# A two-layer decoder trunk on one core: the causal products of the first layer on 64-token pieces and four 64x64 tiles

## The chip, the cores and the metric

The program runs on one core of a Trainium2 chip. The core has a matrix engine (TensorE, "PE" in the profile; its weight loads are listed as "PEld"), a vector engine (VectorE, "DVE"), an activation engine (ScalarE, "ACT"), a general engine (GpSimd, "POOL"), and queues that start DMA transfers from HBM (mostly that of SyncE, "SP"). Each engine works through its own list of instructions in order, and semaphores tie the lists together. The metric is the device time of one execution in microseconds (us), the median of several runs.

## The reference, cut to what matters

256 tokens of width 2048 go through two layers, in float32. The first is a Mamba-2 mixer: a projection gives z, xs, B, C and dt; xs, B and C pass a short convolution and a SiLU. The 64 heads (64 wide) lie in 8 groups of 8 heads; the heads of a group share B and C (128 states). With da the decay per token and head, the output of a head is

```
cb    = C · B^T                                    (256 x 256, one per group)
decay = exp(sum of da over (s, q])   for s <= q    (one per head)
y[q]  = sum over s <= q of cb[q,s] * decay[q,s] * (dt[s] * xs[s])
```

The reference does this in chunks of 128 tokens with a carried state; the kernel forms the causal 256 x 256 products directly. Then follow a skip term, the gate silu(z), a group norm and the output projection. The second layer is sliding-window attention (window 128, 32 query heads over 4 key heads, a sink term), gated and projected out. Both layers end in a layer norm over the residual.

## The kernel before, in words

All weights are streamed once. A unit is 1 MB of a weight matrix: two DMAs (`load_half`, L169), a rounded copy by ACT (`wh`, L178) and the remainder by DVE (`wl`, L181). Every large product is three products of rounded and remainder parts: `mac` (L265) for the projections into z, xs, B, C, q and the gate, and `out_unit` (L339) for the output projections. Units are prepared ahead of their use, in the order of the list `srcs`.

The first layer is a sequence of blocks of 128 columns (`SEQ`): per group the blocks B, C, four of xs, four of z. A plan (`at(t, fn, ...)`, `beside`, `between`) puts the small work of a group behind certain blocks. For group g that is:

- `load_decay` (L534): DMAs that spread the summed decays of four heads over all 128 partitions (tile `rb`). They are issued by POOL for groups 0 to 2 (but one) and by SP after that.
- `sum_decay` (L566) and `exp_decay` (L573), on ACT: the exponent of the decay for each pair of tokens, into tile `e`. Rows (partitions) are the source tokens s of a chunk of 128 and columns are the target tokens q: 256 columns for the first chunk and 128 for the second, 384 per head, 1536 for the four heads of a half group.
- `cb` (L607 and L608): two matmuls, B of a chunk against C, 128x128 stationary, 256 and 128 columns; DVE masks the result into `cbm` (L609).
- `by_cb` (L614), on DVE: `e` times `cbm`, for four heads at once.
- `turn_first` (group 0, L625 and L629) or `turn_xs`, `carry_xs`, `scale_xs` (L641, L651, L657): xs with tokens on partitions, times dt, into tile `xd`.
- `ymm` (L670): for every pair of heads and chunk, `xd` (128 tokens x 64) stationary against `e`. The two heads of a pair go to the two halves of the output partitions, so that two matmuls run on two 128x64 column tiles of PE. DVE takes the result out with a scale (L675) and adds the skip term (L681).
- `gate` (L686 to L701), on POOL, ACT and DVE, then the norm of the group and, a group later, its output projection.

`turn_dt` (L487 to L497) prepares the decays with tokens on partitions (`rtk`, `dtx`). float32 operands that are not in the rounded format take two passes of PE: each such matmul stands in the profile as two instructions.

In the second layer `attend(j, h)` forms the scores (L1209, L1216), DVE and ACT the softmax; `weigh` (L1248 to L1251) and `turn_far` (L1258) divide by the sum and transpose; `rest` calls both. For the pairs (j, h) in `BEHIND_HALF`, `rest` is put off to the next output block. `gate_block` ends each of its blocks with a product on DVE (L1185). At the very end columns 512 to 2047 of rows 0 to 127 are normalised by `norm_aside` on ACT and POOL (L1426 to L1428), and rows 128 to 255 by DVE, ACT and PE (`last`, L1412 to L1447).

PSUM is split into four tiles `mm` and four tiles `ax`, which are handed out in turn.

Of the kernel before, what the change touches and what calls it, by code (L numbers as in the profile page):

```python
# [8 lines left out]
F32 = mybir.dt.float32  # L9
# [61 lines left out]
NSM = 7  # L71
B_ORDER = [("q", 0), ("g", 0), ("q", 1), ("g", 1), ("q", 2), ("o", 0), ("g", 2), ("q", 3),
# [6 lines left out]
BEHIND_HALF = [(1, 1)]  # L79
# [18 lines left out]
def trunk(ctx: ExitStack, tc: tile.TileContext, A: dict, out: bass.AP, dbg=None):  # L98
# [30 lines left out]
    mask_ssd = cc[:, 256:640]  # L129

    tri = cc[:, 256:384]
# [60 lines left out]
    def load_first():  # L192
# [3 lines left out]
        for tag, n in FIRST:  # L196
            if tag == "xr":
                buf = xr_t
            elif tag == "wr":
                buf = wp.tile([P, 1024], F32, tag="wr", name=nm("first"), bufs=NR)  # L200
            else:
                w, bufs = {"rb": (1024, 2), "e": (1536, 2), "yz": (1024, 1)}[tag]
                buf = ap.tile([P, w], F32, tag=tag, name=nm("first"), bufs=bufs)
            raws += [buf[:, i * FW : i * FW + FW] for i in range(n)]
# [209 lines left out]
    dtx = ap.tile([P, 2, NHD], F32, tag="dtx", name="dtx")  # L414
    rtk = ap.tile([P, 2, 2 * NHD], F32, tag="rtk", name="rtk")
# [68 lines left out]
    def turn_dt(sums, dt, q):  # L484
        pt = ax_tile()
        for i, v in enumerate((sums[:, 0, :], sums[:, 1, :], dt)):
            nc.tensor.transpose(pt[:, i * P : (i + 1) * P], v, ident)  # L487
        nc.scalar.copy(
            rtk[:].rearrange("p c (k h) -> p k c h", k=2),
            pt[:, :256].rearrange("p (k c h) -> p k c h", k=2, c=2),  # L490
        )
        elo = q[:]
        nc.scalar.activation(
            elo[:, :128].rearrange("p (c h) -> p c h", c=2), rtk[:, :, 64:128], AF.Exp, scale=-1.0
        )
        nc.vector.tensor_tensor(
            dtx[:], pt[:, 256:384].rearrange("p (c h) -> p c h", c=2),  # L497
            elo[:, :128].rearrange("p (c h) -> p c h", c=2), ALU.mult,
# [30 lines left out]
    def load_decay(g, hf):  # L529
        rb = ap.tile([P, 4, S], F32, tag="rb", name=nm("rb"), bufs=2)  # L530
# [3 lines left out]
        m = (nc.sync if sp else nc.gpsimd).dma_start(  # L534
            rb[:],
            rscr[h0 : h0 + 4, :]
            .rearrange("h q -> (h q)").partition_broadcast(P)
            .rearrange("p (h q) -> p h q", h=4),
        )
        if sp and g < 2:  # L540
            tc.keep_in_program_order(m)
        rbs[g, hf] = rb
# [13 lines left out]
    def sum_decay(g, hf, first=0, last=4):  # L556

        rb = rbs[g, hf]
        h0 = g * 8 + hf * 4
        if first == 0:  # L560
            es[g, hf] = ap.tile([P, 4, 384], F32, tag="e", name=nm("e"), bufs=2)
        e = es[g, hf]
        for h in range(first, last):
            for c, cols in ((0, slice(0, 256)), (1, slice(256, 384))):

                m = nc.scalar.activation(  # L566
                    e[:, h, cols], rb[:, h, c * P :], AF.Relu, scale=-1.0, bias=rtk[:, c, h0 + h : h0 + h + 1]
# [3 lines left out]
    def exp_decay(g, hf):  # L571
        e = es[g, hf]
        m = nc.scalar.activation(e[:], e[:], AF.Exp, scale=-1.0)  # L573
# [29 lines left out]
    def cb(g):  # L603
        st = gs[g]
        cbm = ap.tile([P, 384], F32, tag="cbm", name=nm("cbm"), bufs=1)
        ps = ax_tile()
        nc.tensor.matmul(ps[:, :256], st.bt[:, :128], st.ct[:], start=True, stop=True)  # L607
        nc.tensor.matmul(ps[:, 256:384], st.bt[:, 128:], st.ct[:, 128:], start=True, stop=True)  # L608
        nc.vector.tensor_tensor(cbm[:], ps[:, :384], mask_ssd, ALU.mult)  # L609
        st.cbm = cbm  # L610

    def by_cb(g, hf):
        e = es[g, hf]
        nc.vector.tensor_tensor(e[:], e[:], gs[g].cbm[:].unsqueeze(1).to_broadcast([P, 4, 384]), ALU.mult)  # L614

    def turn_first(g):

        st = gs[g]
        st.xd = ap.tile([P, 2, 4, P], F32, tag="xd", name=nm("xd"), bufs=1)
        for k in range(2):  # L620
# [5 lines left out]
            for i in (2 * k, 2 * k + 1):  # L626
                o = (i % 2) * S
                hh = g * 8 + 2 * i
                m = nc.vector.tensor_tensor(  # L629
                    st.xd[:, :, i, :].rearrange("p c (h d) -> p c h d", h=2),  # L630
                    ps[:, o : o + S].rearrange("p (c h d) -> p c h d", c=2, h=2),
                    dtx[:, :, hh : hh + 2].unsqueeze(3).to_broadcast([P, 2, 2, 64]), ALU.mult,
                )
                pinned(m, True)

    def turn_xs(g):
# [6 lines left out]
        st.xd = ap.tile([P, 2, 4, P], F32, tag="xd", name=nm("xd"), bufs=1)  # L643

    def carry_xs(g, js):

        st = gs[g]
        z = st.zx[:].rearrange("p i (c j) b -> p j c i b", c=2)
        for j in js:
            for i in range(4):  # L650
                m = nc.scalar.copy(st.xd[32 * j : 32 * j + 32, :, :, 32 * i : 32 * i + 32], z[32 * i : 32 * i + 32, j])  # L651
                pinned(m, g > 1 and j > 1)

    def scale_xs(g):
        v = gs[g].xd[:].rearrange("p c i (h d) -> p c (i h) d", h=2)
        d = dtx[:, :, g * 8 : g * 8 + 8].unsqueeze(3).to_broadcast([P, 2, 8, 64])
        pinned(nc.vector.tensor_tensor(v, v, d, ALU.mult), g == 0)  # L657

    def ymm(g):
        st = gs[g]  # L660
        st.yz = ap.tile([P, 4, S], F32, tag="yz", name=nm("yz"), bufs=1)
        for k in range(2):
            ps = ax_tile()
            for i in (2 * k, 2 * k + 1):
                o = (i % 2) * S
                for c in range(2):
                    cols = slice(o + c * P, o + S)
                    for r in range(2):
                        e = es[g, i // 2][:, 2 * (i % 2) + r, :]
                        nc.tensor.matmul(  # L670
                            ps[64 * r : 64 * r + 64, cols], st.xd[:, c, i, 64 * r : 64 * r + 64], e[:, 256:] if c else e[:, :256],
                            start=c == 0, stop=c == 1,
# [902 lines left out]
```

## Time and profile before

| | |
|---|---|
| median of 3 runs | 975.67 us (975.39 to 976.33) |
| the profiled execution | 976.57 us, its span 973.9 us |
| mean granted TensorE clock | 0.997 |
| busy PE / DVE / ACT / POOL | 965.6 / 786.3 / 671.2 / 121.4 us |
| `ymm` on PE (L670) | 256 instructions |
| `cb` on PE (L607, L608) | 32 instructions |

The profile follows one execution. Its chain of waits runs from the last instruction back to whatever released each step, so a time that stands in the chain for a PE group is time that the group adds to the end. The list of waits tells for each engine what it stood still for. A busy time of a group is the sum of what its instructions took and overlaps with others on a pipelined engine; the time in the chain does not.

### The profile page before, as it was taken

How to read it: one execution, taken by the hardware profiler on the slowest of the kernel's cores; microseconds unless marked ns; L12 is line 12 of the kernel's file. 1: busy time of each engine (PE TensorE's matmuls, PEld its weight loads, DVE VectorE, ACT ScalarE, POOL GpSimd, SP SyncE). 2: the span in 40 equal slices, each digit the busy share in tenths (PEclk: the TensorE clock that was granted, in tenths of full speed). 3: DMA queues.
4: the chain of work that ended last, by engine and by line, in shares of the span. 5: the costliest groups of instructions: out<-in, count | busy, mean ns of one | idle time of the engine just before them, and what ended most of it. 6: DMA issues, size and time to landing. Idle time of an engine off the chain costs nothing.

```text
span 973.9 us, 18857 instructions
## 1 busy us (share of the span) xinstructions
PE 965.6 (99%) x7332; PEld 894.5 (92%) x7332; DVE 786.3 (81%) x1216; ACT 671.2 (69%) x1282; POOL 121.4 (12%) x203
## 2 busy tenths in 40 slices
PE   9999999999999999999999999999999999999997
PEld 8999989998999999999899899888999988898976
DVE  7888898886977877787797687889977769778777
ACT  7585883884795685587377579567777776784772
POOL 0000303102110310310300121411000000000003
PEclk9999999999999999999999999999999999999999
DMA  9688566575667666576576654568655545466642
GB/s 357 246 299 323 159 216 227 199 245 189 224 191 226 200 208 205 174 233 203 155 254 201 212 186 158 175 194 266 200 174 155 176 152 174 152 193 196 215 132 86
DMA packets 61273, 197.90 MB, mean 203 GB/s; under 512 B 6800, under 2 KB 11328, under 8 KB 60928
## 3 DMA queue, kind: packets, MB, share of 16 engines
q1 hardware_dynamic: 58528, 188.53, 58.9%
q0 software_dynamic: 2048, 7.65, 2.4%
q8 instruction: 57, 0.93, 0.4%
q10 hardware_dynamic: 608, 0.52, 0.2%
q14 instruction: 32, 0.26, 0.1%
HBM read 194.45 MB, written 2.23 MB: 202 GB/s over the span
## 4 chain that ended last, share of the span: by engine, by line
PE 93%; DVE 4%; ACT 2%; issue 1%; DVEq 0%; ACTq 0%
PE mm L265 60%; PE mm L339 25%; PE ax L670 2%; PE mm L1052 2%; DVE wl L181 1%; ACT p L1244 1%; PE ax L607 0%; ACT wh L178 0%; PE mm L406 0%; ACT ptw L1277 0%; ACT pt L1277 0%; PE ax L983 0%; DVE t L1412 0%; PE ax L1209 0%; PE ax L388 0%
## 5 line engine op out<-in xcount | busy, mean ns | idle before, releaser
L181 DVE TENSOR_TENSOR wl<-wr,wh 128x1024 fp32r<-128x1024 f32 (+2 forms) x354 | 391.8, 1127 | 88.2 <-ACT wh L178 86.6
L178 ACT ACTIVATE wh<-wr 128x1024 fp32r<-128x1024 f32 (+2 forms) x354 | 332.8, 974 | 94.9 <-PE mm L265 51.7
L265 PE MATMUL mm<-xH,wh 128*128 128x256 f32 x1280 | 355.4, 278 | 0.0
L265 PE MATMUL mm<-xL,wh 128*128 128x256 f32 x1280 | 354.4, 277 | 0.0
L265 PE MATMUL mm<-xH,wl 128*128 128x256 f32 x1280 | 354.4, 277 | 0.0
L265 PEld LDWEIGHTS mm<-xH,wh 128*128 128x128 f32 x1280 | 240.7, 188 | 1.8 <-issue 0.5
L265 PEld LDWEIGHTS mm<-xL,wh 128*128 128x128 f32 x1280 | 240.6, 188 | 1.0
L265 PEld LDWEIGHTS mm<-xH,wl 128*128 128x128 f32 x1280 | 240.4, 188 | 0.0
L265 PE MATMUL mm<-x1H,wh 128*128 128x256 f32 x512 | 143.1, 280 | 2.1 <-DVE sg L1185 2.1
L265 PE MATMUL mm<-x1L,wh 128*128 128x256 f32 x512 | 142.6, 278 | 0.0
L265 PE MATMUL mm<-x1H,wl 128*128 128x256 f32 x512 | 142.4, 278 | 0.0
L339 PE MATMUL mm<-wh,yH 128*128 128x512 f32 x256 | 100.7, 394 | 0.0
L265 PEld LDWEIGHTS mm<-x1H,wh 128*128 128x128 f32 x512 | 96.9, 189 | 3.6 <-DVE sg L1185 2.4
L339 PE MATMUL mm<-wl,yH 128*128 128x512 f32 x256 | 99.8, 390 | 0.0
L339 PE MATMUL mm<-wh,yL 128*128 128x512 f32 x256 | 99.8, 390 | 0.0
L265 PEld LDWEIGHTS mm<-x1H,wl 128*128 128x128 f32 x512 | 97.0, 190 | 0.0
L265 PEld LDWEIGHTS mm<-x1L,wh 128*128 128x128 f32 x512 | 96.9, 189 | 0.1
L510 DVE SCALAR_TENSOR_TENSOR cv<-mm,pc,cv 128x255 f32<-128x255 f32 x144 | 68.4, 476 | 4.6 <-ACT cv L508 2.5
L686 POOL TENSOR_TENSOR yz<-yz,z 128x256 f32<-128x256 f32 x32 | 26.7, 842 | 259.9 <-DVE yz L681 259.9
L339 PEld LDWEIGHTS mm<-wl,yH 128*128 128x128 f32 x256 | 48.1, 188 | 10.2
L339 PEld LDWEIGHTS mm<-wh,yH 128*128 128x128 f32 x256 | 48.1, 188 | 9.3 <-issue 0.3
L339 PEld LDWEIGHTS mm<-wh,yL 128*128 128x128 f32 x256 | 48.1, 188 | 9.0
(246 smaller groups left out, 1264.4 us busy)
## 6 DMA issues: line engine op xcount, KB each, us to landing
wr<-in_wa SPq DMA_DIRECT2D x154, 512.0 KB, 5.2
wr<-in_wo SPq DMA_DIRECT2D x64, 512.0 KB, 4.5
wr<-in_wq SPq DMA_DIRECT2D x32, 512.0 KB, 4.4
wr<-in_wg SPq DMA_DIRECT2D x31, 512.0 KB, 5.2
wr<-in_wb SPq DMA_DIRECT2D x16, 512.0 KB, 3.8
wr<-in_wb SPq DMA_DIRECT2D x32, 256.0 KB, 4.3
rb<-rscr SPq DMA_DIRECT2D x11, 512.0 KB, 5.3
wr<-in_wkv SPq DMA_DIRECT2D x8, 512.0 KB, 6.0
```

The costliest lines, as they stand in the source:

```text
L178: m = nc.scalar.activation(h[:, sl], v, AF.Copy)
L181: m = nc.vector.tensor_tensor(l[:, sl], v, h[:, sl].bitcast(F32), ALU.subtract)
L265: m = nc.tensor.matmul(ps, a, b, start=first and i == 0, stop=last and i == 2)
L339: pinned(nc.tensor.matmul(ps, a[:, k, hs], (u.h, u.l)[l][:, ks], start=n == 0 and add is None, stop=n == 11), pin)
L510: nc.vector.scalar_tensor_tensor(a[:, sft:], ps[:, : S - sft], w(3 - sft), a[:, sft:], ALU.mult, ALU.add)
L670: nc.tensor.matmul(ps[64 * r : 64 * r + 64, cols], st.xd[:, c, i, 64 * r : 64 * r + 64], e[:, 256:] if c else e[:, :256], start=c == 0, st ...
L686: nc.gpsimd.tensor_tensor(v, v, st.z[i][:], ALU.mult)
L1052: m = nc.tensor.matmul(ps[:], (x1H, x1L, x1H)[i][:, kk, hs], (u.h, u.h, u.l)[i][:, ks], start=(kk, i) == (0, 0), stop=ui == 3 and (k, i) = ...
L1244: nc.scalar.activation(byhead[:, r], byhead[:, r], AF.Exp, bias=ng[:, r : r + 1], accum_out=rs[:, r : r + 1])
```

## The change

The pieces of tokens become 64 long in the first layer. Even pieces (0 and 2) of one member of a head pair and odd pieces lie on opposite partition halves, and for the other member the other way round: tile `e` holds, on each half of the partitions, the 256, 192, 128 and 64 columns of four pieces for two heads (1280 columns instead of 1536).

- `ymm`: 32 matmuls per group instead of 16, each with 64 rows and 64 output rows, so that four 64x64 tiles of PE are in use; the results lie in two PSUM tiles by row half, and both are taken out after all matmuls. The gates go in the order 0, 2, 1, 3.
- `cb`: four matmuls with 64 stationary columns; the products land on the partition half of their piece. DVE masks them in two steps of 64 partitions, and POOL copies each half to the other partition half.
- `load_decay`: two DMAs onto 64 partitions each instead of one onto 128, half the bytes; the tile holds a whole group.
- `turn_dt`: four copies of 64 partitions instead of one of 128, and a small second set of scales (`dtq`) for group 0. `turn_first`: eight products of 64 partitions instead of four of 128. `carry_xs` and `scale_xs`: the same number and size of instructions to other places.
- Second layer: `rest` of attend(3, 0) is put off behind the first gate product of block 3, which is held ahead of it on DVE. At the end, the multiplication of columns 1536 to 2047 of rows 0 to 127 goes from POOL to DVE, behind the statistics of (1, 1), and the addition on POOL after it.

```diff
+PART = [slice(a, a + 256 - 64 * c) for c, a in enumerate((0, 320, 512, 256))]
-BEHIND_HALF = [(1, 1)]
+BEHIND_HALF = [(1, 1), (3, 0)]
...
-        nc.scalar.copy(
-            rtk[:].rearrange("p c (k h) -> p k c h", k=2),
-            pt[:, :256].rearrange("p (k c h) -> p k c h", k=2, c=2),
-        )
...
+        for r, i in ((0, 0), (1, 1), (0, 1), (1, 0)):
+            to = rtk[64 * r : 64 * r + 64, i].rearrange("p k c n -> p (k c n)").rearrange("p (m b) -> p m b", b=2)
+            of = pt[64 * i : 64 * i + 64, :384].rearrange("p (m r b) -> p r m b", r=2, b=2)[:, r]
+            if r == i:
+                nc.vector.tensor_copy(to, of)
+            else:
+                nc.scalar.copy(to, of)
...
     def load_decay(g, hf):
-        rb = ap.tile([P, 4, S], F32, tag="rb", name=nm("rb"), bufs=2)
+        if hf == 0:
+            rbs[g] = ap.tile([P, 2, 2, S], F32, tag="rb", name=nm("rb"), bufs=2)
...
+        for r in range(2):
+            m = (nc.sync if sp else nc.gpsimd).dma_start(
+                rbs[g][64 * r : 64 * r + 64, hf],
+                rscr[h0 + 2 * r : h0 + 2 * r + 2, :]
...
+        for b in range(first // 2, last // 2):
+            n = 4 * g + 2 * hf + b
+            for c in range(4):
                 m = nc.scalar.activation(
-                    e[:, h, cols], rb[:, h, c * P :], AF.Relu, scale=-1.0, bias=rtk[:, c, h0 + h : h0 + h + 1]
+                    e[:, b, PART[c]], rbs[g][:, hf, b, 64 * c :], AF.Relu, scale=-1.0,
+                    bias=rtk[:, c % 2, 0, c // 2, n : n + 1],
...
-        nc.tensor.matmul(ps[:, :256], st.bt[:, :128], st.ct[:], start=True, stop=True)
-        nc.tensor.matmul(ps[:, 256:384], st.bt[:, 128:], st.ct[:, 128:], start=True, stop=True)
-        nc.vector.tensor_tensor(cbm[:], ps[:, :384], mask_ssd, ALU.mult)
+        for c, half, to in ((0, 0, 0), (1, 64, 0), (2, 64, 192), (3, 0, 256)):
+            nc.tensor.matmul(
+                ps[half : half + 64, to : to + 256 - 64 * c], st.bt[:, 64 * c : 64 * c + 64], st.ct[:, 64 * c :],
+                start=True, stop=True,
+            )
+        for r in range(2):
+            rows, at = slice(64 * r, 64 * r + 64), slice(320 * r, 320 * r + 320)
+            nc.vector.tensor_tensor(cbm[rows, at], ps[rows, :320], mask_ssd[rows], ALU.mult)
+        for r in range(2):
+            rows, at = slice(64 * r, 64 * r + 64), slice(320 * r, 320 * r + 320)
+            nc.gpsimd.tensor_copy(cbm[64 - 64 * r : 128 - 64 * r, at], cbm[rows, at])
...
-                m = nc.vector.tensor_tensor(
-                    st.xd[:, :, i, :].rearrange("p c (h d) -> p c h d", h=2),
...
+                for q in range(2):
+                    rows = slice(64 * q, 64 * q + 64)
+                    m = nc.vector.tensor_tensor(
+                        to[:, q], ps[rows, o : o + S].rearrange("p (c h d) -> p c h d", c=2, h=2),
...
+        pss = [ax_tile(), ax_tile()]
         for k in range(2):
-            ps = ax_tile()
...
+            for c in range(4):
+                for r in range(2):
+                    rows = slice(64 * r, 64 * r + 64)
+                    for b in range(2):
                         nc.tensor.matmul(
-                            ps[64 * r : 64 * r + 64, cols], st.xd[:, c, i, 64 * r : 64 * r + 64], e[:, 256:] if c else e[:, :256],
-                            start=c == 0, stop=c == 1,
+                            pss[r][64 * b : 64 * b + 64, k * S + 64 * c : k * S + S], st.xd[rows, k, b, c],
+                            es[g, k][rows, b, PART[c]], start=c == 0, stop=c == 3,
...
-        for i in range(4):
+        for i in (0, 2, 1, 3):
             at(y, gate, g, i)
...
-            nc.vector.scalar_tensor_tensor(
+            m = nc.vector.scalar_tensor_tensor(
                 t[:, p_, :], t[:, p_, :], 1.0, ps[:, :S], ALU.add, ALU.mult
             )
+            pinned(m, bool(behind_gate))
+            while behind_gate:
+                behind_gate.pop()()
...
-            halves.append(rest)
+            (behind_gate if j == 3 else halves).append(rest)
...
-        ordered(nc.scalar.activation(v, v, AF.Identity, scale=sc[h][1][:], bias=nmr[:]))
-        ordered(nc.gpsimd.tensor_tensor(v, v, gb2[0][:, cols(nb)], ALU.mult))
+        if nmr is not None:
+            ordered(nc.scalar.activation(v, v, AF.Identity, scale=sc[h][1][:], bias=nmr[:]))
+            if nb == 3:
+                return
+        ordered((nc.vector if nb == 3 else nc.gpsimd).tensor_tensor(v, v, gb2[0][:, cols(nb)], ALU.mult))
...
+        elif (h, nb) == (1, 1):
+            norm_aside(0, 3, None)
```

More of the change, by code (lines that the diff above doesn't have):

```diff
@@ L411, in first_products @@
         return pss
-    dtx = ap.tile([P, 2, NHD], F32, tag="dtx", name="dtx")
-    rtk = ap.tile([P, 2, 2 * NHD], F32, tag="rtk", name="rtk")
+    dtx = ap.tile([P, NHD // 2, 4], F32, tag="dtx", name="dtx")
+    dtq = ap.tile([P, 2, 2, 8], F32, tag="dtq", name="dtq")
+    rtk = ap.tile([P, 2, 3, 2, NHD // 2], F32, tag="rtk", name="rtk")
     rscr = dram.tile([P, S], F32, tag="rscr", name="rscr")
@@ L556, in sum_decay @@
     def sum_decay(g, hf, first=0, last=4):
-        rb = rbs[g, hf]
-        h0 = g * 8 + hf * 4
         if first == 0:
-            es[g, hf] = ap.tile([P, 4, 384], F32, tag="e", name=nm("e"), bufs=2)
+            e = ap.tile([P, 1408], F32, tag="e", name=nm("e"), bufs=2)
+            es[g, hf] = e[:, :1280].rearrange("p (h q) -> p h q", h=2)
         e = es[g, hf]
-        for h in range(first, last):
-            for c, cols in ((0, slice(0, 256)), (1, slice(256, 384))):
+        for b in range(first // 2, last // 2):
+            n = 4 * g + 2 * hf + b
+            for c in range(4):
                 m = nc.scalar.activation(
-                    e[:, h, cols], rb[:, h, c * P :], AF.Relu, scale=-1.0, bias=rtk[:, c, h0 + h : h0 + h + 1]
+                    e[:, b, PART[c]], rbs[g][:, hf, b, 64 * c :], AF.Relu, scale=-1.0,
+                    bias=rtk[:, c % 2, 0, c // 2, n : n + 1],
                 )
@@ L1146, in trunk @@
     halves = []
+    behind_gate = []
     def rotate(q):
```

81 lines of the change are left out of this document (37 added, 44 removed).

## The prediction

> **What bounds the kernel now.** I read the page first, then the list of what PE waited for.
>
> ```profile
> span 973.9 us, 18857 instructions
> ...
> PE 965.6 (99%) x7332; PEld 894.5 (92%) x7332; DVE 786.3 (81%) x1216; ACT 671.2 (69%) x1282; POOL 121.4 (12%) x203
> ...
> PE 93%; DVE 4%; ACT 2%; issue 1%; DVEq 0%; ACTq 0%
> ```
>
> ```profile
> PE mm L265 <- DVE sg L1185: 2.1, 1, 2.1
> ```
>
> PE is the bound nearly everywhere: it makes up 93% of the chain, and its one wait inside the span is 2.1 us, on the gate product L1185 in the second layer. In the first layer PE waits for nothing, so there only PE's own time counts, unless the change makes a wait. The rows that price it come from the chain of waits in order of time (start, duration, what), where a duration is what a group adds to the end.
>
> ```profile
> 42.85 16.35 PE mm L265 x144
> 59.20 0.43 PE ax L607 x2
> 59.85 16.35 PE mm L265 x144
> ...
> 87.97 2.75 PE ax L670 x32
> 90.72 16.54 PE mm L265 x144
> 107.27 0.34 PE ax L724 x4
> 107.61 0.54 PE ax L607 x2
> ...
> 124.74 5.46 PE mm L265 x48
> ...
> 231.97 2.75 PE ax L670 x32
> 234.72 0.63 PE ax L607 x2
> 235.57 5.47 PE mm L339 x24
> ...
> 732.52 1.46 PE ax L1216 x32
> ...
> 918.35 16.34 PE mm L339 x72
> ```
>
> **Prices of a pass.** L607 is one 256-column matmul of group 0 in two passes: 0.43/2 = 0.216 us a pass. The two 128-column passes of L608 fill the gap behind it: 59.85 - 59.20 - 0.43 = 0.22, 0.110 each. The line through both (0.83 ns a column) gives 0.163 us for 192 columns and 0.057 for 64.
>
> Two column tiles run abreast: 16 passes of 256 and 16 of 128 in pairs make 8 x 0.216 + 8 x 0.110 = 2.61 us, and L670 shows 2.75. Four 64x64 tiles run abreast too: L1216 of the second layer has 32 passes of 192 columns on four tiles; 32/4 x 0.163 = 1.30, and the row has 1.46. What is over, 0.14 and 0.16, is the entry into the tiled state. The way back to the full array costs about 0.20: the 144 matmuls behind L670 take 16.54 against 16.35, and L607 right behind L670 takes 0.63 against 0.43.
>
> **The change, part by part.**
>
> *ymm.* 64 passes per group on four tiles are 16 rounds, four each of 256, 192, 128 and 64 columns: 4 x (0.216 + 0.163 + 0.110 + 0.057) = 2.18, and 0.16 for the entry, 2.34 us instead of 2.75. Eight groups: -3.28 us. Only the 64-column round has no row. Its lower end is the 0.057 of the line; its upper end is that of a 128-column pass, 0.110, near what one-column matmuls behind a 128-wide weight load take (L724, 0.34/4 = 0.085). I take 0.057, since the weight load is half as wide here; the upper end would add 8 x 4 x 0.053 = 1.70.
>
> *cb.* The old pair costs 0.43 + 0.22 = 0.65 in groups 0 and 2, 0.54 + 0.22 = 0.76 in group 1, and 0.63 + 0.22 = 0.85 in groups 3 to 7, where it stands behind ymm and holds the way back. The new one runs on two column tiles, another state than the 64x64 tiles before it, so an entry (0.14) stands before it and the way back (0.20) behind it. In between, pieces 0 and 1 (256 and 192 columns) run side by side, then 2 and 3 (128 and 64); with the passes issued in order the second pass of piece 1 starts with that of piece 0, at 0.216, ends at 0.379, and piece 2 adds 0.220: 0.60. Sum 0.94. Groups 3 to 7: 5 x 0.09; 0 and 2: 2 x 0.29; 1: 0.18; together +1.21 us. Ends: 0.54 if the halves run freely (2 x 0.216 + 2 x 0.057 = 0.546 on one), 0.77 if the two passes of one matmul come before those of the next; no entry at all between the two tiled states at best. That makes +0.03 to +2.57.
>
> *The work beside it.* ACT's and DVE's passes over `e` shrink from 1536 to 1280 columns and the bytes of `rb` halve; no PE wait hangs on them, so this brings nothing. What is added is 8 small products instead of 4 in `turn_first` and two copies more on DVE in `turn_dt`. The first set stands here:
>
> ```profile
> 80.49 1.41 DVE L629 TENSOR_TENSOR xd<-ax,dtx 128x256 f32<-128x256 f32 x4
> ```
>
> Four more at 0.35 make 1.4 us on DVE; the tile is ready at 81.9 and would be at 83.3, and ymm starts at 87.97: hidden. Uncovered, it would be 1.4. The four copies of `turn_dt`, at the same 0.35 on two engines, fall in a stretch where PE runs 144 matmuls from 42.85 without a gap. The second DMA of each `load_decay` queues behind its first on SP or POOL with half the bytes, and its tile no longer waits for the ACT of the half group before. The outgoing ymm results reach DVE only when all rounds are done, up to half of 2.34 later in PE's terms, and POOL's gates start after the two `cbm` copies: the only reader is the output projection a group later (in group 7, which has no copies, three output units later). All taken at nothing.
>
> The tight place is group 1, where `by_cb` stands right behind `cb` on DVE and now waits for POOL's copies:
>
> ```profile
> 119.17 0.55 DVE L609 TENSOR_TENSOR cbm<-ax,cc 128x384 f32<-128x384 f32 x1
> 119.64 0.74 DVE L348 SCALAR_TENSOR_TENSOR xr<-mm,r,xr 128x512 f32<-128x512 f32 x1
> 120.30 1.75 DVE L614 TENSOR_TENSOR e<-e,cbm 128x1536 f32<-128x1536 f32 x1
> 121.97 0.75 DVE L348 SCALAR_TENSOR_TENSOR xr<-mm,r,xr 128x512 f32<-128x512 f32 x1
> 122.63 2.35 DVE L181 TENSOR_TENSOR wl<-wr,wh 128x1024 fp32r<-128x1024 f32 x2
> ```
>
> ```profile
> 117.64 0.55 POOL L534 DMA_DIRECT2D rb<-rscr  x1 [6.50 <-ACT e L566]
> L850 POOL CAST xH<-xH 128x256 fp32r<-128x256 f32 x1 | 1.1, 1105 | 0.0
> ```
>
> Behind `by_cb` stand two halves of weights (L181); the first is done at 123.8 and used by the matmuls from 124.74, a spare of 0.9. A POOL copy costs at most the 1.1 us of L850, the dearest near row: masking (0.45 for its first half) and two copies end 2.65 us after 119.17, 1.52 later than `by_cb` started; it is itself 0.29 shorter (256 of 1536 columns). The weights come up to 1.23 late, PE waits 0.0 to 0.4. I take 0: ACT and DVE have less to do just before.
>
> *The two waits in the second layer.* The wait of 2.1 us is in block 2, and the reordered one in block 3. What L1185 of block 3 does there:
>
> ```profile
> 905.40 0.42 DVE L1185 SCALAR_TENSOR_TENSOR sg<-sg,mm 128x256 f32<-128x256 f32 x1
> ```
>
> It frees one of four `mm` tiles in turn; three more gate blocks pass, and the tile is wanted at 918.35, 12.5 us later. An earlier L1185 helps nobody. What goes behind it, `rest` of attend(3, 0), feeds only products that come after three more output units. Price 0 both ways.
>
> At the end, the chain runs through DVE, and there is a delay:
>
> ```profile
> 956.93 0.75 DVE L1412 SCALAR_TENSOR_TENSOR t<-xr,mv,gb 128x512 f32<-128x512 f32 x1
> 962.00 0.69 DVE L350 TENSOR_TENSOR xr<-xr,mm 128x512 f32<-128x512 f32 x1 [0.90 <-PE mm L339]
> 965.91 1.31 DVE L1412 SCALAR_TENSOR_TENSOR t<-xr,mv,gb 128x512 f32<-128x512 f32 x1
> ```
>
> ```profile
> 965.41 1.27 POOL L1428 TENSOR_TENSOR xr<-xr,gb 128x512 f32<-128x512 f32 x1
> ```
>
> The same instruction takes 0.75 alone and 1.31 while POOL's last addition runs until 966.68. With one multiplication less, POOL is done some 1.3 us earlier, before 965.91; the multiplication fits DVE's idle 0.90 before 962.00 (0.69, as L350); it waits for the third of ACT's three scalings, and L350 of the next columns queues behind it. SP's stores keep their order, and the one concerned leaves earlier. That is -0.56; the lower end is 0, if DVE and POOL get in each other's way there.
>
> **Sum.** -3.28 + 1.21 - 0.56 = -2.63 us on the profiled 976.57 (span 973.9 and 2.67 around it), 973.9. The median of the runs shown is 0.9 below the profiled execution; from it, 975.67 - 2.63 = 973.0. All good ends give -3.28 + 0.03 - 0.56 = -3.81 (971.9), all bad ones -3.28 + 1.70 + 2.57 + 0.4 = +1.4 (977.1).
>
> **Rivals.** (a) The passes in cb do not pair: 8 x 0.17 more, 974.4. Every case of two tiles in the trace has equal columns; none shows 256 beside 192.
>
> [...]
>
> (c) Slower: `by_cb` of group 1 waits not only for the copies but for what stands before them in POOL's queue. The issue of L534 above waited 6.50 us for ACT. If such a wait precedes the copies, the weights come 6.5 - 0.9 - 0.29 = 5.3 us late, and after a stop PE is slow as well:
>
> ```profile
> 835.00:838.50 3.50, 3.50 (x19) 3.50 (x19) 2.00 (x2) 3.41 (x9) 0.00 (x0) 0.52 0.74 247
> ```
>
> In this window behind the 2.1 us wait the granted clock was 0.52, with 19 matmuls where 31 fit at 16.35/144 each: 1.4 us lost. Together 973.0 + 5.3 + 1.4 = 979.7. It decides from a wait of 3.2 us on (4.6 with the clock: 2.63 to undo and 1.95 beyond). Against it: `rb` has a tile for each group now, so the issue has nothing to wait for.
>
> (d) The wait of block 2 goes after all, with its slow clock: 2.1 + 1.4 less, 969.5. Nothing in the change touches attend(2, 0).
>
> **How the numbers follow.** The sum has a chance of 0.66 (its own range 972.0 to 974.0, of it 0.60 past the bound), (a) 0.11, (b) 0.06, (c) 0.11, (d) 0.04, and 0.02 for a smaller loss elsewhere. 0.2% is 1.95 us, about what a measurement here can tell from no change. Faster is 0.60 + 0.04; the same (973.7 to 977.6) is 0.06 from the sum with (a) and (b); slower is (c) and the rest. The range 971.3 to 975.4 leaves out (c) and (d) and holds (a) and (b).
>
> **What would show it.** L670's successor at 2.3 us per group in the chain, x64; the cb lines at about 0.74 behind it and the next group 0.2 longer; no PE wait near 120 to 130; the 2.1 us wait unchanged; the first L1412 at the end at 0.75. Wrong would be: rounds of the 64x64 tiles longer than the line, or a new PE wait.

## The result, and the profile after

The changed kernel is slower: 980.4 us median of 7 runs (978.22 to 981.65), against 976.06 of the kernel before on the same chip. The ratio is 1.004, with a 95% interval of 1.0031 to 1.005. The forecast was 973.0. The profiled execution took 981.65 us, the longest of the 7; its span is 6.0 us longer than that of before (973.9), where the medians differ by 4.3.

The page of after, its first line, the busy times, and the engines' shares of the chain that ended last:

```profile
span 979.9 us, 19511 instructions
...
PE 968.3 (99%) x7620; PEld 898.6 (92%) x7620; DVE 791.5 (81%) x1232; ACT 664.9 (68%) x1284; POOL 124.7 (13%) x223
...
PE 82%; DVE 5%; issue 4%; DMA 4%; ACT 3%; POOL 1%; ACTq 0%; SPq 0%; DVEq 0%; POOLq 0%
```

PE was 93% of the chain before and is 82% now; DMA, which had no share, has 4%. The list of what PE waited for shows where (total, times, longest):

```profile
PE ax L741 <- POOL sq L709: 2.5, 1, 2.5
PE mm L265 <- DVE sg L1203: 2.0, 1, 2.0
PE mm L265 <- DVE wl L181: 1.1, 1, 1.1
```

The wait on the gate product (L1203, L1185 before) is the old one. Two are new: the norm of group 0 (L741, L724 before) waits for POOL's gate products, and a block near 52 us waits for its weights. The chain of waits of after, followed back from 130 us in order of time (start, duration, what), tells how they hang together:

```profile
44.77 6.48 DMA wr<-in_wa
...
52.23 0.41 ACT ct L519
...
55.20 7.29 DMA wr<-in_wa
...
70.33 0.39 DVE cbm L619
...
111.29 0.74 POOL sq L709
112.03 0.04 issue
112.08 1.02 PE ax L741 x4
113.09 1.26 PE ax L613 x6
114.35 7.61 PE mm L339 x24
```

Before, PE itself was this chain from 42 us on. Now two weight loads (`wr`) of 6.5 and 7.3 us stand in it, DVE's `cbm` of group 0 comes at 70.33, and POOL's last square ends at 112.03, when PE has been standing for 2.5 us. Behind the stop, the product of B and C (L613) takes 1.26 us and the 24 matmuls of L339 take 7.61; in group 3 and after they take 0.69 and 5.67. The granted clock behind the stop is in the windows of after (stretch, its length; then busy time and number of instructions on PE, PE's weight loads, DVE, ACT and POOL; granted clock, DMA share, GB/s):

```profile
45.00:50.00 5.00, 5.00 (x47) 5.00 (x46) 3.17 (x6) 1.78 (x2) 4.00 (x7) 1.00 0.94 238
50.00:55.00 5.00, 4.11 (x37) 3.91 (x35) 2.27 (x4) 3.20 (x6) 0.00 (x0) 1.00 1.04 319
...
112.00:116.00 4.00, 3.92 (x16) 3.41 (x17) 3.52 (x5) 0.35 (x2) 0.02 (x1) 0.50 0.61 186
```

The same windows of before:

```profile
45.00:50.00 5.00, 5.00 (x47) 5.00 (x46) 5.00 (x10) 4.28 (x8) 0.00 (x0) 1.00 0.96 385
50.00:55.00 5.00, 5.00 (x47) 5.00 (x46) 3.63 (x5) 4.31 (x9) 0.00 (x0) 1.00 1.07 321
```

The DMA engines are as busy in both, 0.94 and 0.96 of their time at 45 to 50 us, but they moved 238 GB/s instead of 385 there; at 50 to 55 us the rates are equal. ACT worked 1.78 us instead of 4.28 in the first stretch, DVE 2.27 instead of 3.63 in the second. The waits of after between 40 and 62 us name it:

```profile
ACT wh L178 <- DMA wr<-in_wa: 5.7, 4, 4.5
DVE ct L520 <- ACT ct L519: 4.5, 1, 4.5
```

ACT stood 4.5 us for one weight buffer; the longest such wait of before in this stretch is 1.7. The activation of `ct` is queued behind that weight half on ACT, and DVE's next work behind `ct`.

The parts that were priced came out like this, in the chain of after between 140 and 245 us, and near its end:

```profile
149.26 2.34 PE ax L686 x64
...
184.53 0.69 PE ax L613 x6
185.22 11.51 PE mm L265 x96
...
242.69 0.69 PE ax L613 x6
```

```profile
972.04 2.09 DVE t L1433 x3
```

The whole difference of 6.0 us between the two profiled executions, from the ends of the matmuls in both traces (stretch by stretch between the same neighbours) and from the last rows of DVE:

| part | forecast, us | measured, us |
|---|---|---|
| ymm, 8 groups (2.75 to 2.34 each) | -3.28 | -3.28 |
| cb with its entry and the way back | +1.21 | +0.83 |
| DVE's scalings at the end (2.65 to 2.09) | -0.56 | -0.56 |
| slower pace: 144 + 96 matmuls in group 0, 96 in group 2 | 0 | +1.42 |
| block near 52 us waits for weights (16.35 to 17.70) | 0 | +1.35 |
| stop before the norm of group 0 (0.34 to 3.49) | 0 | +3.15 |
| half clock behind the stop (L613 and L339) | 0 | +2.5 |
| start, last store and small pieces | 0 | +0.6 |

What the sum priced came to -3.01 us, better than the -2.63 forecast. What it took at nothing cost 9.0 us, nearly all of it in the first two groups.

### The profile page after: what moved, and what is told of

Its sections match the earlier page's. It is cut to its first block, busy times and chain, and to the rows that moved or that the text cites. A ratio compares the mean times of both kernels' runs of the same rounds, so it can differ in the third digit from the quotient of the medians.

```text
span 979.9 us, 19511 instructions
## 1 busy us (share of the span) xinstructions
PE 968.3 (99%) x7620; PEld 898.6 (92%) x7620; DVE 791.5 (81%) x1232; ACT 664.9 (68%) x1284; POOL 124.7 (13%) x223
## 4 chain that ended last, share of the span: by engine, by line
PE 82%; DVE 5%; issue 4%; DMA 4%; ACT 3%; POOL 1%; ACTq 0%; SPq 0%; DVEq 0%; POOLq 0%
PE mm L265 51%; PE mm L339 25%; DMA wr<-in_wa 2%; PE mm L1069 2%; DVE wl L181 2%; PE ax L686 2%; ACT wh L178 1%; DMA xr<-in_first 1%; ACT p L1265 1%; PE ax L613 1%; DMA first<-in_first 1%; PE ax L1237 0%; ACT ptw L1298 0%; PE ax L1000 0%; PE ax L1230 0%
## 5 line engine op out<-in xcount | busy, mean ns | idle before, releaser
L339 PE MATMUL mm<-wh,yH 128*128 128x512 f32 x256 | 101.6, 397 | 0.0
L339 PE MATMUL mm<-wh,yL 128*128 128x512 f32 x256 | 100.5, 393 | 0.0
L339 PE MATMUL mm<-wl,yH 128*128 128x512 f32 x256 | 100.5, 393 | 0.0
L717 ACT ACTIVATE yH<-yz,pc 128x256 fp32r<-128x256 f32 x32 | 16.3, 510 | 70.2 <-POOL yz L703 70.2
L339 PEld LDWEIGHTS mm<-wl,yH 128*128 128x128 f32 x256 | 48.5, 189 | 10.3
L339 PEld LDWEIGHTS mm<-wh,yH 128*128 128x128 f32 x256 | 48.6, 190 | 9.9
```

Source lines behind the costliest of these rows:

```text
L339: pinned(nc.tensor.matmul(ps, a[:, k, hs], (u.h, u.l)[l][:, ks], start=n == 0 and add is None, stop=n == 11), pin)
L717: nc.scalar.activation(yH[:, i, :], v, AF.Copy, scale=pc[:, c : c + 1])
```

## The experiments

Two theories of the late weights stood at the start. Theory 1: the loads of group 1's decay rows, which no longer wait for ACT, run on POOL's queue at 47 us and take the DMA engines from the weights. This is their row in the timeline of after (start, length of all, what):

```profile
46.94 2.06 POOL L540 DMA_DIRECT2D rb<-rscr  x4
```

Before, the first load of group 1 was issued at 60.5, after 15.6 us of waiting, the end of it for ACT (timeline of POOL in before):

```profile
60.50 0.53 POOL L534 DMA_DIRECT2D rb<-rscr  x1 [15.62 <-ACT e L566]
```

Theory 2: SP issues the weights later, because the loads of group 0 stand ahead of them in its queue, two now instead of one: 44.77 in this profile against 42.63 before.

**e1_hold: group 1's loads held back**

```diff
-            nc.gpsimd.tensor_copy(cbm[64 - 64 * r : 128 - 64 * r, at], cbm[rows, at])
+            st.turned = nc.gpsimd.tensor_copy(cbm[64 - 64 * r : 128 - 64 * r, at], cbm[rows, at])
...
+    def hold_decay(g, hf):
+        with tc.issue_after(gs[0].turned.ins): load_decay(g, hf)
...
-            at(10, load_decay, 1, 0)
-            at(10, load_decay, 1, 1)
+            at(10, hold_decay, 1, 0)
+            at(10, hold_decay, 1, 1)
```

> The changed kernel with one move: the four POOL loads of the second group's decay rows are queued behind POOL's two copies of cbm of the first group (about 70 us) instead of running from 46.9 to 49. Theory 1 (these loads, which no longer wait for ACT, take the DMA engines from the weights at 45 to 55 us): ACT's wait for a weight buffer near 47 us falls from 4.5 us to under 1.5, cbm of the first group returns from 70.3 to about 65, the 2.5 us wait of L741 goes, and the time is 973 to 975. Theory 2 (the weights are late because SP issues them 2 us later, behind the two loads of the first group): ACT still waits 3 us or more, L741 still waits, 979 to 980.5.

975.89 us median of 10 runs (974.2 to 977.47), ratio to before 1.0001 (0.9991 to 1.001). Apart from these loads no engine's order is changed, and 4.5 us are back. The chain of waits of e1_hold, whose profiled execution is the fastest of the 10, is PE again:

```profile
59.06 0.69 PE ax L613 x6
59.75 17.16 PE mm L265 x144
76.91 0.87 PE ax L638 x8
77.78 11.31 PE mm L265 x96
89.09 2.34 PE ax L686 x64
91.43 16.54 PE mm L265 x144
107.97 0.34 PE ax L741 x4
```

L741 takes 0.34 as before. The waits of ACT for weight buffers between 40 and 62 us are

```profile
ACT wh L178 <- DMA wr<-in_wa: 2.6, 2, 2.0
```

so the longest is 2.0 us (4.5 in after; under 1.5 was expected), and DVE's `cbm` of group 0 starts at 64.1 instead of 70.3. Theory 1 holds. The median stayed above the 973 to 975 expected; two reasons follow below.

**e2_sp_late and e3_both: the loads of group 0, two steps later in the program**

```diff
-            at(4, load_decay, 0, 1)
+            at(6, load_decay, 0, 1)
```

> The changed kernel with one move: SP's two loads of the first group's second half of decay rows stand six weight loads later in SP's queue (two steps of the program later), so that no weight load waits for the write of rscr. Theory 2: the weight loads are issued from about 42 us instead of 44.8, ACT's wait near 47 us falls to under 1.5 and the time is 973 to 975. Theory 1: POOL's early loads still collide, the wait stays at 2.5 us or more, 978 to 980.5.

> Both moves together. Theories 1 and 2 alike: no wait of ACT over 1.5 us near 47, no wait at L741, 972.5 to 974.5. A third theory (the first group's products, gates and copies alone are too late for L741, whatever the loads do): the wait of L741 stays at 1.5 us or more with the slow matmuls behind it, and the time stays at 976 or more.

This edit did not do what its name says: the planner put the two loads at the same place in SP's queue, and the order of every engine is that of the changed kernel (e2) and of e1_hold (e3). They are repeats of those two: 979.99 us (979.07 to 980.62, ratio 1.0041) and 975.93 us (974.72 to 978.24, ratio 0.9999). The repeat still settles theory 2, because in the profile of e2_sp_late the write of `rscr` landed earlier, and the weights were issued as early as before, by the timeline of SP's queue:

```profile
41.24 1.15 SPq L540 DMA_DIRECT2D rb<-rscr  x2
42.49 3.86 SPq L169 DMA_DIRECT2D wr<-in_wa  x4
```

With the weights issued at 42.49 ACT stood for them 7.7 us in all (5 times) and L741 waited 2.9 us. The moment of issue is not the cause; theory 2 falls. So does the third theory, of e3_both: L741 takes 0.34 there as in e1_hold. The rate at 45 to 50 us is 303 GB/s in e2_sp_late and 342 in e1_hold, so the 238 of after is in part the later issue of that execution; what separates the two kernels is how long ACT stands for its weights.

**e4_second: the kernel before with the second layer's edits alone**

```diff
-BEHIND_HALF = [(1, 1)]
+BEHIND_HALF = [(1, 1), (3, 0)]
...
+            pinned(m, bool(behind_gate))
+            while behind_gate:
+                behind_gate.pop()()
...
-            halves.append(rest)
+            (behind_gate if j == 3 else halves).append(rest)
...
-        ordered(nc.gpsimd.tensor_tensor(v, v, gb2[0][:, cols(nb)], ALU.mult))
+        ordered((nc.vector if nb == 3 else nc.gpsimd).tensor_tensor(v, v, gb2[0][:, cols(nb)], ALU.mult))
```

> The kernel before with the two reorderings of the second layer alone. All theories: the first layer is that of before, the first DVE scaling at the end takes 0.75 us instead of 1.31, the wait of 2.1 us in block 2 stays; 0.5 to 0.6 us faster than before, 975.5. If the reordering of the wait in block 3 costs something of its own it is slower than before.

975.21 us (974.35 to 975.96), ratio 0.9989 (0.998 to 0.9999). The row at the end of its chain, beside 2.65 before:

```profile
966.09 2.09 DVE t L1416 x3
```

The wait of 2.1 us in block 2 stays. The tail's -0.56 is confirmed, and the second layer has no part in the loss.

**e6_dummy: the loads without the change**

The kernel before, with four loads of 64 partitions on POOL's queue at 44.8 to 46.3 us, into a tile that nothing reads (the free `yz` buffer):

```diff
+    def load_more():
+        t = ap.tile([P, 4, S], F32, tag="yz", name=nm("more"), bufs=1)
+        for i in range(4):
+            r, hf = i % 2, i // 2
+            nc.gpsimd.dma_start(
+                t[64 * r : 64 * r + 64, 2 * hf : 2 * hf + 2, :],
+                rscr[8 + 2 * i : 10 + 2 * i, :].rearrange("h q -> (h q)").partition_broadcast(64).rearrange("p (h q) -> p h q", h=2),
+            )
...
             at(4, load_decay, 0, 1)
+            at(4, load_more)
```

> The kernel before, all its work unchanged, with four more loads on POOL's queue of the same kind, size and place as the changed kernel's early loads of the second group (64 partitions by two rows of 1 KB each from rscr), into a tile that nothing reads. Theory 1 (these loads by themselves delay the weights at 45 to 55 us): ACT waits 3 us or more for a weight buffer there, the first group's cbm comes some 4 us later than its 64.1, the norm of the first group waits 1 to 3 us for POOL's gates, and the time is 978 to 981. The rival (the loads hurt only together with the changed kernel's own added work on DVE in that group): no wait at the norm, 976 to 977.

979.01 us (977.53 to 981.58), ratio 1.0033 (1.002 to 1.0046). From the waits of e6_dummy, those of PE and then those of all engines between 40 and 62 us:

```profile
PE ax L731 <- POOL sq L699: 2.8, 1, 2.8
...
ACT wh L178 <- DMA wr<-in_wa: 7.2, 2, 3.8
```

This is the chain of events of the changed kernel, without any tile of the array changed: the weights late, the norm of group 0 (here L731) waiting for POOL's gates, the slow clock behind it (0.66 at 109 to 113 us). The rival, that the loads hurt only beside the change's own DVE work, falls. They cost 2.9 us here and 4.5 in the changed kernel; that they hurt more beside that DVE work would fit, but no run separates it.

**e11_dummy_one: the same bytes in one load**

```diff
-        for i in range(4):
-            r, hf = i % 2, i // 2
-            nc.gpsimd.dma_start(
...
+        nc.gpsimd.dma_start(
+            t[:], rscr[8:12, :].rearrange("h q -> (h q)").partition_broadcast(P).rearrange("p (h q) -> p h q", h=4)
+        )
```

> The kernel of e6_dummy with its four loads of 64 partitions by 2 KB made one load of 128 partitions by 4 KB: the same 512 KB on the same queue at the same place, one issue instead of four. If the bytes alone delay the weights: the same loss as e6_dummy, 978.5 to 980. If the loss comes from the many short rows and issues: less than half of it, 976 to 977.5, with the DMA engines over 330 GB/s at 45 to 55 us.

977.7 us (975.69 to 981.21), ratio 1.0021 (1.0008 to 1.0034): between the two expectations, with a wide spread. In its profile the DMA engines moved 395 GB/s at 45 to 50 us, against 349 in e6_dummy, and the norm waited 0.5 us. The bytes alone cost something; four loads of half the partitions seem to cost more, but the intervals overlap, in the profiled executions the one load went out at 43.1 us and the four at 44.8, and the split between the two is not settled. The mean time of a packet of 4 KB, from the DMA records, shows what happens while such loads run:

```
                weight packets in 1 us, ns each   POOL's packets, ns each   KB in 1 us
before, 50-51 us        102, 162                        0                       418
after,  53-54 us         39, 238                       25, 251                  262
```

While the loads of 64 partitions run, each packet takes about half as long again and the rate falls by 37%. The packet time alone does not prove that these loads are the reason: in e1_hold, with no load of POOL running, packets of 4 KB take 178 to 231 ns between 54 and 60 us. Beside the load of 128 partitions in e11_dummy_one the packets took 159 to 181 ns at 365 to 438 KB in 1 us (45 to 50 us); but that load differs in the number of issues and the length of its rows as well, so no run here isolates the partitions.

**e5_wide_last: the slower pace**

In e1_hold's chain above, 144 matmuls take 17.16 us and 96 take 11.31, where 16.54 (with the way back) and 10.90 were expected: 0.1178 us each instead of 0.1136, at a granted clock of 1.00 and with no wait. It is the same to 0.01 us in after, e1, e2, e3. e5 is e1_hold with

```diff
-        for c, half, to in ((0, 0, 0), (1, 64, 0), (2, 64, 192), (3, 0, 256)):
+        for c, half, to in ((3, 0, 256), (2, 64, 192), (1, 64, 0), (0, 0, 0)):
```

> The kernel of e1_hold with the four pieces of the product of B and C issued in the reverse order: 64, 128, 192, 256 columns. Under e1_hold the 256-column matmuls behind the first group's product take 0.1178 us each instead of 0.1136, 240 of them until the 64x64 tiles come, and 96 more behind the third group's. Theory A (the slower pace is a state that narrow last passes on a column tile leave behind): with the wide piece last the pace is 0.1136, 0.61 + 0.41 + 0.41 = 1.4 us less than e1_hold, the time about 0.15% under it. Theory B (two column tiles as such leave it, or what runs beside): 0.1178 stays and the time is that of e1_hold.

975.76 us (974.29 to 976.33), ratio 0.9997 (0.9987 to 1.0006), and the same 17.16, 11.31 and 11.50 (behind the third group's product). Theory A falls: the order of the pieces has no part in it. Theory B was only that the pace stays, and does not say which of its two causes it is.

**e7_gate2: the wait in block 2**

e1_hold with

```diff
-BEHIND_HALF = [(1, 1), (3, 0)]
+BEHIND_HALF = [(1, 1), (2, 0), (3, 0)]
...
-            (behind_gate if j == 3 else halves).append(rest)
+            (behind_gate if j > 1 else halves).append(rest)
```

> The kernel of e1_hold with the reordering of the wait done for block 2 as well: the softmax rest of attend(2, 0) stands behind the first gate product of block 2. The wait of 2.1 us of L265 on the gate product and the half clock behind it (1.4 us) go: 3.5 us less than e1_hold, about 972.4. The rival (the rest comes late for its own products and a wait moves there): 975 or more, with a new PE wait behind block 2.

977.43 us (976.19 to 978.06), ratio 1.0009 (1.0 to 1.0019), 1.5 us more than e1_hold. The wait on the gate product is gone, and this one stands in the list of PE's waits:

```profile
PE mm L339 <- DVE xr L350: 1.9, 1, 1.9
```

The rival holds: the wait moved. 288 matmuls behind the old place took 33.66 us instead of 35.27, the 72 of L339 behind them 18.80 instead of 16.34.

**e8_turn_act: less work on DVE in group 0**

e1_hold with `turn_first` in four products of 128 partitions into the free `yz` buffer and eight ACT copies:

```diff
-                for q in range(2):
-                    rows = slice(64 * q, 64 * q + 64)
-                    m = nc.vector.tensor_tensor(
-                        to[:, q], ps[rows, o : o + S].rearrange("p (c h d) -> p c h d", c=2, h=2),
-                        dtq[rows, 1, :, 2 * i : 2 * i + 2].unsqueeze(3).to_broadcast([64, 2, 2, 64]), ALU.mult,
-                    )
-                    pinned(m, True)
+                m = nc.vector.tensor_tensor(
+                    by[:, i], ps[:, o : o + S].rearrange("p (c h d) -> p c h d", c=2, h=2),
+                    dtq[:, 1, :, 2 * i : 2 * i + 2].unsqueeze(3).to_broadcast([P, 2, 2, 64]), ALU.mult,
+                )
+                pinned(m, True)
+                for q in range(2):
+                    nc.scalar.copy(to[:, q], by[64 * q : 64 * q + 64, i])
```

> The kernel of e1_hold with the first group's products of turn_first done by four DVE products of 128 partitions into a spare tile and eight ACT copies from there, instead of eight DVE products of 64 partitions: DVE has some 2 us less to do before the first group's gates, ACT some 2.5 more. Theory 3 (DVE's added work in the first group leaves no spare, and single runs lose 1 to 3 us to a short wait there): the runs lie closer together and the median falls by 1 to 1.5 us against e1_hold, 974.4 to 975. The rival (DVE's added work has its place, ACT is as tight): 976 or more.

974.81 us (974.54 to 977.33), ratio 0.999 (0.998 to 0.9999). 6 of 10 runs lie under 974.9, against 1 of 10 of e1_hold. That is the expected direction and size, but the two intervals overlap; e13 below tests the same cause with a larger ablation.

**e9_again, e10_long, e12_long2: what ends the slow pace**

e9 is e8 with other operand places at the first matmuls behind cb; e10 is e8 with one pass of 512 columns, its result not read, behind cb of groups 0 and 2; e12 adds the same pass behind `turn_first`:

```diff
 e9
-    visits = (turn_dt, cb, turn_first, ymm, norm)
+    visits = (turn_dt, turn_first, ymm, norm)
 e10, in cb
+        if g in (0, 2):
+            nc.tensor.matmul(ax_tile()[:].rearrange("p (k s) -> p k s", k=2), xL(1, 2)[:, 0, :P], xH(1, 3), start=True, stop=True)
 e12, in turn_first, behind the transposes
+            if k == 1:
+                nc.tensor.matmul(ax_tile()[:].rearrange("p (k s) -> p k s", k=2), xL(1, 2)[:, 0, :P], xH(1, 3), start=True, stop=True)
```

> The kernel of e8_turn_act with one word less: cb is no longer among the visits after which the next block takes the first piece of xH and xL from its own place instead of from the copy beside the others. Theory P1 (the pace of 0.1178 us is set by the operands' places at the first matmuls behind the two-tile product): the 144 and 96 matmuls behind the first group's product and the 96 behind the third's go at 0.1136, 1.4 us less than e8_turn_act. Theory P2 (the two column tiles leave the pace, whatever the next operands): 0.1178 stays, the time is that of e8_turn_act.

> The kernel of e8_turn_act with one more matmul of 512 columns on the full array, its result not read, behind the product of B and C of the first and the third group. Theory P3 (the slow pace is a state that lasts until a pass of 512 columns, as behind the third group's product, where it ends with the output unit): the pace behind it is 0.1136; 1.4 us less and 2 x 0.23 more, about 0.95 us less than e8_turn_act. If another thing ends it, 0.1178 stays and it is 0.45 us longer.

> The kernel of e10_long with a third matmul of 512 columns on the full array, its result not read, behind the eight transposes of turn_first. If a pass of 512 columns ends the slow pace wherever it comes from: the 96 matmuls behind turn_first go at 0.1136 (10.90 instead of 11.31 us), no stretch of the first layer at 0.1178 is left, and the time is 0.18 us less than e10_long. As the changed kernel with its loads held back, DVE relieved and the pace kept, it should lie 1 to 2 us under the kernel before: 974 to 975. If the pace there has another cause: 11.31 stays.

975.5 us (ratio 0.9998, 0.9988 to 1.0007), 974.78 us (0.9987, 0.9977 to 0.9996) and 975.6 us (0.9996, 0.9987 to 1.0005). The times missed what was expected: the median of e10 is level with that of e8 instead of 0.95 us under it, and that of e12 is 0.8 above e10 instead of 0.18 under it. What the passes did is read from the traces alone. The chain of waits of e9:

```profile
60.24 17.17 PE mm L265 x144
77.41 0.87 PE ax L638 x8
78.28 10.92 PE mm L265 x96
```

The stretches, from the ends of the matmuls (us; the way back from two column tiles, 0.20, is inside the first and the third; before has none there, and in e10 and e12 it falls on the added pass):

```
                                   before   after, e1, e5, e8   e9      e10     e12
144 behind the first group's cb    16.35    17.16              17.16   16.36   16.36
 96 behind turn_first              10.90    11.31              10.92   11.31   10.91
 96 behind the third group's cb    10.90    11.50              11.50   10.91   10.91
```

Other operand places changed one stretch of three, and not the one right behind them: P1 falls as stated. A pass of 512 columns, put in at these three places, kept the slow pace from following, at 0.235 us each. That is what P3 says, but P3 is not the whole rule; two findings speak against it. In e1_hold a slow stretch stands directly behind 24 matmuls of 512 columns (L339):

```profile
125.59 5.67 PE mm L265 x48
```

The same 48 take 5.75 in e12 and e10, and 5.47 in after and e13. And in before, behind L1216, the pace goes back from 0.1178 to 0.1136 at 788.9 us, between two blocks of 256 columns, with no wider pass. So a wider pass is neither enough nor needed. Whether the width, the other operands or the pass as such worked at the three places is not shown, and what sets the pace stays open.

**e13_less_dve: where the gain goes**

With these three slow stretches gone e12 was no faster than e1_hold. In its profile PE has a wait in the first layer that e1_hold's has not:

```profile
PE mm L265 <- DVE cv L514: 1.4, 1, 1.4
```

It is at 115 us, and PE loses 1.65 us at it. The kernel of e1_hold has it too, in other executions; e3_both, the same order of work, shows

```profile
PE mm L265 <- DVE cv L514: 1.2, 1, 1.2
```

and loses 1.4 us there. This is most of the 2.0 us between the profiled executions of e1_hold (974.2) and e3_both (976.23). e13 is e12 with group 0's four additions of D times x left out:

```diff
-            for i in (r, r + 2):
+            for i in (r, r + 2) if g else ():
```

> The kernel of e12_long2 with the first group's four additions of D times x left out (the output lacks them): 4 DVE instructions, some 2.6 us of DVE at 97 to 101, behind which the weights and the second group's blocks queue. Theory D (with the loads held back, the first two groups are bound by DVE, so that what PE saves there comes back as a wait of L265 for DVE near 115): the wait of 1.4 us and the slow clock behind it go, the runs lie closer together, and the median is 1.2 to 2 us under e12_long2, 973.6 to 974.4. The rival (the wait near 115 comes from the weight loads, not from DVE's work): it stays, 975 or more.

973.78 us (973.37 to 974.42), ratio 0.9979 (0.997 to 0.9989): the lowest of the series (with less work done), and the narrowest spread. Its chain of waits is PE without a gap from 55 to 125 us; some of its rows:

```profile
61.05 16.36 PE mm L265 x144
...
78.28 0.24 PE ax L642
78.52 10.91 PE mm L265 x96
...
109.34 5.67 PE mm L339 x24
115.02 5.46 PE mm L265 x48
```

DVE was busy 10.80 of the 15 us from 90 to 105, against 13.82 in e12 and 14.21 in e1_hold. Theory D holds in its main part: with the loads held back, the first two groups are bound by DVE nearly as much as by PE, and the wait at 115 us is the price of DVE's work. That it takes back just what PE gains is not shown, since e3_both has the wait with the slow pace still in it. Nor does DVE's work set it alone: in e12 the chain that ends in the wait goes back through DVE and ACT to a weight load at 53.87 us that takes 5.02 us.

No version that does all the work reached the forecast. e10_long, at 974.78, is the best of them, level with e8_turn_act: about 0.1% under the kernel before, 0.5% under the changed one.

## Why the prediction was wrong

**The step that failed** is *The work beside it*, and in it one sentence: the second DMA of each `load_decay` "queues behind its first on SP or POOL with half the bytes, and its tile no longer waits for the ACT of the half group before", taken at nothing. The wait for ACT had been holding the two loads of group 1 (512 KB each) back until 60.5 and 71.1 us, past the stretch in which the DMA engines are full; with it gone the loads that replace them (four, 512 KB in all) went out at 47 us, ACT stood for its weights, and PE for the gates of group 0. e1_hold gives the price: 4.5 us. e6_dummy shows that the loads do it by themselves. The windows of before, quoted above, have the DMA engines at 0.96 and 1.07 of their time there; the prediction has no such row. The prediction used the lost wait as an argument against rival (c), and never asked what the earlier transfers would meet.

**Terms that held.** ymm at 2.34 us in all eight groups; the round of four 64-column tiles took the 0.057 of the line (one start of 0.036 and three of 0.007). Rival (b), 0.06 of the chances, stands for longer 64-column rounds; no run shows a term that makes them longer, and in before, too, four matmuls of L1216 on four tiles lie within 0.39 us (732.45), while one takes 0.326 on average. The tail at -0.56, alone in e4_second as well. The way back at 0.20. The wait of 2.1 us unchanged, so rival (d) did not come; e7_gate2 shows that its price would not have been won. Of the 1.4 us that (d) adds for the slow clock, 1.0 is given back at the end, as the last section shows. No wait of `by_cb` near 120 to 130, so rival (c) had the wrong place and the wrong cause, a wait of POOL's copies; late weights and the slow clock behind a stop it had right. That its 979.7 lies near the measured 980.4 is luck.

**Terms that were mis-sized.** The eight small products of `turn_first` take 3.55 us on DVE in e1_hold, 2.1 more than the four of before; 1.4 more was forecast. *cb*: 0.69 instead of 0.74 for entry and stream. The two column halves run freely (0.14 + 0.55), which was the lower end given; rival (a) falls.

**What was missing.** The pace behind cb: 1.42 us. The trace of before held a case: the 96 matmuls from 782.94, behind L1216, take 11.31 us; of the 0.41 above 10.90 half is the way back, and half is that the first 48 go at 0.1178 each. The prediction prices the way back and asks nothing of the pace behind it. And DVE's added 2 us in group 0 were called hidden because the next reader came 4.7 us later; the spare of that tile was right, but the spare of DVE as a whole, which the later blocks' weights and gates draw on, was smaller than that: between 40 and 110 us DVE is busy 65.0 of 70 us in e1_hold, 62.2 in before. e13_less_dve shows it: taking 2.6 us from DVE there brings the median down by 1.8.

## What to carry to other kernels

A wait that a change removes may have been keeping a transfer out of a full stretch: before pricing it at nothing, find the time at which the transfer will now run, and read the DMA share and GB/s there. A spare has to be taken for the whole queue of an engine, up to the next place where PE waits for it, not for the one tile that is looked at. Where two engines are nearly level, test the gain on one with an ablation on the other (here 4 DVE instructions) before looking for another cause.

## What the hardware did that was not expected

- Two paces at full clock: the 256-column matmuls go at 0.1136 or 0.1178 us each. The slower one begins behind matmuls of another shape and was kept for 48, 96 or 144 matmuls; one pass of 512 columns prevented it at three places, but 24 such passes of L339 did not at 125.6 us of e1_hold. What sets it is open.
- Stops and the clock. The 2.5 us stop of after was followed by a granted clock of 0.50 (row 112 to 116 above), the 1.4 us stop of e12 by 1.00. Behind the same 2.1 us wait, where before had 0.52, the windows of e1_hold show

```profile
835.00:838.50 3.50, 3.50 (x32) 3.50 (x31) 1.60 (x4) 3.41 (x10) 0.00 (x0) 1.00 0.75 232
```

  with 35.27 us for the 288 matmuls of that block instead of 36.66. So the half clock comes in some executions and not in others of about the same stop. It costs 1.4 us where it comes, but the execution that is spared it gives 1.0 back at the end, where the last 120 matmuls of L339 wait for DVE (27.18 instead of the 26.14 of after); about 0.4 us is left for the spread between runs. Executions of the same kernel differ as well: of the 25 runs of before that were taken beside e1_hold, 10 have a mean granted clock of 1.0 and 15 one of 0.997 or 0.998. The half clock stands behind stops of 2.1 us (before, 0.52) and 2.5 us (after, 0.50); what decides whether it comes no run here shows.
